# The delta rule's scan in chunks of 128 tokens instead of 64, its triangle's inverse doubled once more, the decays' mask as a factor

## The chip, the cores and the metric

The kernel runs on one core of one Trainium2 chip. The metric is the device time of one execution in microseconds (us); before the change it is 1946.99 us, the median of three runs (1946.99 to 1947.81). The engines are called TensorE (PE in the profile, PEld for its weight loads), VectorE (DVE), ScalarE (ACT), GpSimd (POOL) and SyncE (SP, a DMA queue).

## The reference, cut to what matters

The program is four layers one after another over 512 tokens of width 1024: two of attention and long convolution, then two hybrid layers. Each hybrid layer has three branches: a gated delta rule with 4 heads of 128x128 state, a latent attention with 8 heads, and a linear recurrence (LRU). Only the delta rule is touched by the change:

```python
def gated_delta_rule(q, k, v, g, beta):      # chunks of C = 64 tokens in the reference
    gc = cumsum(g) within the chunk
    decay = exp(where(tril, gc[i] - gc[j], -inf))
    a_mat = where(strict_tril, (k*beta) @ k.T * decay, 0) + eye(C)
    u, w = triangular_solve(a_mat, [v*beta, k*beta*exp(gc)])
    attn = where(tril, q @ k.T * decay, 0)
    for each chunk n:
        v_new = u - w @ state
        o     = (q * exp(gc)) @ state + attn @ v_new
        state = state * exp(g_last) + (k * exp(g_last - gc)).T @ v_new
```

The result does not depend on the chunk's length in exact arithmetic: a longer chunk means a larger triangle to invert and fewer steps of the loop.

## The kernel before, in words

Tokens lie in 4 tiles of 128 partitions (index i), heads are c = 0 to 3. A projection is 8 x 3 matmuls of 512 columns (lines 261 to 263, `mm3`: high and low parts of the operands), and accumulates in one of three PSUM buffers, which `ps("acc")` hands out in turn as acc, acc, fl (lines 233 to 244). Other PSUM tags are lg (2 buffers), tr and ft (1 each, in turn) and av (1). Big SBUF tiles of 128x4x512 come from `U()`, one pool whose number of buffers is the first argument of `k.pools(10, dict(acc=2, fl=1, lg=2, tr=1, ft=1, av=1))` (lines 222 and 1591). Weights pass through `wchunk`: one DMA on SyncE, a copy on ScalarE (line 269), a difference on VectorE or GpSimd (line 270), three buffers of each.

The order on each engine is not written out by hand. A planner (Tile) takes the instructions in program order as priorities, simulates the engines and lets an instruction whose operands and buffers are ready go ahead of earlier ones that wait; the queues then run in that fixed order. A tile takes a buffer of its pool when the planner lets its first writer go, and gives it back after its last reader.

A hybrid layer (`layer2`, line 1502) runs in program order:

- `mla_pre` (line 1010) makes the compressed keys `ckv` (a U tile) and the decays' logarithms g.
- `gdn_front` (line 1242): `sums` and `decay` make exp of the decays in `an`: a product of the mask `ml` with g on GpSimd (line 1266), an fp32 matmul by `ms` (1268), a second matmul that adds `negr`, which is -1e30 outside the 64x64 triangles (1269), and an exponential on ScalarE (1270). Then 12 projections make k2, q2 and v2 (U tiles), with a convolution on VectorE (`conv4`, line 990) and, for the keys, scales on GpSimd (1289 to 1295) and the triangle `at` (1305).
- `solve32` (line 1356), placed in the program before the last query projection: the sixteen 32x32 diagonal blocks go to DRAM and back (ScalarE's DMA queue, 1360 and 1364) into a U tile `w`, whose second half is cleared on GpSimd (1365); 31 steps of two VectorE instructions invert all blocks (1371, 1373); the result goes to DRAM (`dm`, 1374), its transpose is made on ScalarE (1375) and goes to DRAM too (`dmt`, 1376).
- `spread` (line 1384): twelve DMAs on ScalarE's queue bring the inverted blocks back as `xc` and `xtc` (two tiles tagged "go") and on the diagonal of `XT` (cleared on GpSimd, 1390).
- `gdn_inv` (line 1398), per tile of 128 tokens: two products on TensorE (1406, 1412) with copies on ScalarE (1408, 1414) make the off-diagonal 32x32 block of each 64x64 triangle; then `wt` and `un` (1418, 1422).
- `gdn` (line 1430): the gate `gz`, a U tile, is made of four projections, each emptied by a tanh on ScalarE and a product on VectorE (`silu2`, lines 703 and 704). Then the scan: for each tile i and each half n of 64 tokens, per pair of heads q: two matmuls by the state (1462), a difference on VectorE (1463), two for the queries (1465), two for the state's update (1470), the decayed state on GpSimd (1473) and its sum on VectorE (1474). After both halves `later` and the tile's output (1479 to 1497).
- `lru` (line 1174): per c a projection with a convolution (987, 990), gates through av (1204, 1207), a scan, a second projection and the output `o`, a U tile, written on GpSimd (1223).
- `mla_v`, `mla`, then `out2`.

Of the kernel before, what the change touches and what calls it, by code (L numbers as in the profile page):

```python
# [51 lines left out]
def shape_constants():  # L52
    c = {}
    i = np.arange(256)
    cas = lambda w: np.stack([np.cos(w) + np.sin(w), np.cos(w) - np.sin(w)], 1)
    m = np.arange(P)
    th = np.pi * (4 * i + 1) / 2048
    ph = 2 * np.pi * (((2 * m[:, None] + 1) * (4 * i[None, :] + 1)) % 2048) / 2048
    fwd = cas(ph)
    c["fwd"] = np.stack(_f32r(fwd))  # L60
    f = np.where(i < P, np.cos(th), np.sin(th)) ** 2 / 1024.0
    inv = (fwd * f).reshape(P, 2, 2, P).transpose(3, 2, 1, 0)
    c["inv"] = np.ascontiguousarray(inv, np.float32)
    d = np.concatenate([np.arange(q, S, 4) for q in (0, 2, 1, 3)])
    w = 2 * np.pi * ((m[:, None, None] * 2 + np.arange(2)[:, None]) * (4 * m + 1) % 1024) / 1024
    flt = np.stack(_f32r(np.stack([np.cos(w), np.sin(w)], 2)))
    c["fltb"] = flt.reshape(2, P, 4, P)
    c["rot"] = np.stack([np.tan(th[:P]), -np.tan(th[:P]), 1.0 / np.tan(th[P:]), np.cos(2 * th[:P]), np.sin(2 * th[:P])],
                        1).astype(np.float32)
    tt = np.arange(S, dtype=np.float32) * np.float32(1 / 511)  # L70
    tres = np.arange(S, dtype=np.float32)
    f = np.linspace(1e-4, 15, 16, dtype=np.float32)
    ang = ((np.float32(2.0 * math.pi) * tres)[:, None] * f[None, :]) / np.float32(S)
    z = np.concatenate([tt[:, None], np.cos(ang), -np.sin(ang)], axis=-1).astype(np.float32)
    c["zt"] = np.ascontiguousarray(z[d].T)
    c["negt"] = np.ascontiguousarray(-tt[d].reshape(4, P).T)
    kill = np.zeros((P, 1), np.float32)
    kill[0, 0] = NEG
    c["kill"] = kill
    rel = np.arange(-511, 512)  # L80
    n = np.abs(rel)
    large = 7 + sum((n >= v).astype(np.int64) for v in (8, 12, 16, 23, 32, 46, 64, 91))
    bucket = np.where(rel > 0, 16, 0) + np.where(n < 8, n, large)
    onehot = np.zeros((32, 1024), np.float32)
    onehot[bucket, 1022 - np.arange(1023)] = 1.0
    c["onehot"] = onehot
    ang = np.arange(S, dtype=np.float32)[:, None] * np.array(ROPE_INV, np.uint32).view(np.float32)[None, :]
    co, si = np.cos(ang.astype(np.float64)).T, np.sin(ang.astype(np.float64)).T
    c["cos"] = np.concatenate([co] * 4).astype(np.float32)
    c["sin"] = np.concatenate([-si, si, -si, si]).astype(np.float32)  # L90
    p = np.arange(P)
    same = (p[:, None] // 64) == (p[None, :] // 64)
    le = p[:, None] <= p[None, :]
    c["ml"] = (same & le).astype(np.float32)
    c["ms"] = (same & (p[:, None] > p[None, :])).astype(np.float32)
    c["mc"] = np.stack([np.repeat((p // 64 == n)[:, None], P, 1) for n in range(2)], 1).astype(np.float32)
    c["neg"] = np.where(same & le, 0.0, NEG).astype(np.float32)
    i, j = p[None, :] >> 5, p[:, None] >> 5
    c["lv"] = (((i >> 1) == (j >> 1)) & (i & 1 == 1) & (j & 1 == 0)).astype(np.float32)
    c["causal"] = np.concatenate([np.zeros((P, 384)), np.where(le.T, 0.0, NEG)], 1).astype(np.float32)  # L100
    return c

# [69 lines left out]
class Kern:  # L172
# [789 lines left out]

    def setup2(self):
        nc, A = self.nc, self.A
        for n, shape in (("ml", [P, P]), ("ms", [P, P]), ("mc", [P, 2, P]), ("lv", [P, P])):
            setattr(self, n, self.load(self.cq, n, shape))
        self.negr = self.cq.tile([P, P], F32R, tag="negr", name="negr")
        nc.gpsimd.dma_start(self.negr, A["neg"])
        self.idr = self.cq.tile([P, P], F32R, tag="idr", name="idr")
        nc.scalar.activation(self.idr, self.ident, AF.Copy)  # L970
        self.ones = self.cq.tile([P, 1], F32, tag="ones", name="ones")
        nc.gpsimd.memset(self.ones, 1.0)
        d = lambda n: [self.dp.tile([64, 1024], F32, tag=f"{n}{l}", name=f"{n}{l}") for l in range(2)]
        self.da, self.dm, self.dmt = d("da"), d("dm"), d("dmt")
# [267 lines left out]
    def gdn_front(self, l, h, gab):  # L1242
# [10 lines left out]

        kn, kbt = self.T("XT", four), self.T("X", four)
        quad = lambda n, tag: self.sm(4 * n, tag).rearrange("p (i c) -> p i c", i=4)
        eg, sc, rk, ssq = quad(16, "eg"), quad(16, "sc"), quad(4, "rk"), quad(4, "ssq")
        ones = self.ones
        nc.gpsimd.tensor_scalar(sc[:, :, 12:16], bt, 0.5, None, op0=MUL)
        by = lambda t: t.unsqueeze(2).to_broadcast([P, 4, P])
        tile = lambda i: slice(i * P, (i + 1) * P)  # L1260
# [2 lines left out]
        def decay(i):  # L1263

            rg = self.T("g2", (P, 4, P))
            nc.gpsimd.tensor_tensor(rg, self.mbc(self.ml), self.bc(g[:, i]), op=MUL)
            pd = self.ps("lg", (P, 4, P))
            mm(pd, self.ms, rg, start=True, stop=False)
            mm(pd, self.idr, self.mbc(self.negr), start=False, stop=True)
            nc.scalar.activation(an[:, i], pd, AF.Exp)  # L1270

        def sums():

            pg = self.ps("lg", (P, 4, 16))
            for n, m in enumerate((self.ml, self.ms, self.mc[:, 0], self.mc[:, 1])):
                mm(pg[:, n], m, g.rearrange("p i c -> p (i c)"), start=True, stop=True)
            nc.scalar.activation(eg.rearrange("p i (n c) -> p n i c", n=4), pg.rearrange("p n (i c) -> p n i c", i=4), AF.Exp)

        def keys(c, sq):
            pk = self.ps("tr", (P, 4, P))  # L1280
# [103 lines left out]
    def spread(self, l):  # L1384


        nc = self.nc
        xc, xtc = (self.T("go", (P, 16, 32)) for _ in range(2))
        XT = self.T("XT", (P, 4, 4, P))
        nc.gpsimd.memset(XT, 0.0)  # L1390
        for k in range(4):
            rs = slice(32 * k, 32 * k + 32)
            nc.scalar.dma_start(xc[rs], self.blk(self.dm[l], k))
            nc.scalar.dma_start(xtc[rs], self.blk(self.dmt[l], k))
            nc.scalar.dma_start(self.diag(XT, k), self.blk(self.dmt[l], k))
        return xc, xtc, XT

    def gdn_inv(self, i, at, t1, X, kb, v2):

        nc = self.nc  # L1400
        mm = nc.tensor.matmul
        ts = slice(i * P, (i + 1) * P)
        xc, xtc, XT = X
        p1 = self.ps("lg", (P, 4, 32))
        for c in range(4):
            mm(p1[:, c], at[:, i, c], xc[:, 4 * i + c], start=True, stop=True)
        for b in (0, 64):
            nc.scalar.activation(t1[b + 32:b + 64, i, :, b:b + 32], p1[b + 32:b + 64], AF.Copy)
        yield
        p2 = self.ps("tr", (P, 4, 32))  # L1410
        for c in range(4):
            mm(p2[:, c], t1[:, i, c], xtc[:, 4 * i + c], start=True, stop=True)
        for b in (0, 64):
            nc.scalar.activation(XT[b:b + 32, i, :, b + 32:b + 64], p2[b:b + 32], AF.Copy, scale=-1.0)
        yield
        pw = self.ps("lg", (P, 4, P))
        for c in range(4):
# [12 lines left out]
    def gdn(self, l, h, q2, k2, v2, at, an, kb, egs, ssq, t1, X):  # L1430
# [19 lines left out]
        for i in range(4):  # L1450
            ts = slice(i * P, (i + 1) * P)
            eg = egs[:, i]
            po = self.ps("tr", (P, 4, P))
            for n in range(2):
                rs = slice(64 * n, 64 * n + 64)
                cs = slice(i * P + 64 * n, i * P + 64 * n + 64)
                for q in range(2):
                    hs = slice(2 * q, 2 * q + 2)
                    s1 = st[q]
                    ps = self.ps("lg", (P, 2, P))  # L1460
                    for c in range(2):
                        mm(ps[rs, c], wt[:, i, 2 * q + c, rs], s1[:, c], start=True, stop=True)
                    nc.vector.tensor_tensor(un[rs, hs, ts], un[rs, hs, ts], ps[rs], op=SUB)
                    for c in range(2):
                        mm(po[rs, 2 * q + c], q2[:, 2 * q + c, cs], s1[:, c], start=True, stop=True)
                for q in range(2):
                    hs = slice(2 * q, 2 * q + 2)
                    pS = self.ps("lg", (P, 2, P))
                    for c in range(2):
                        mm(pS[:, c], kd[rs, 2 * q + c, ts], un[rs, 2 * q + c, ts], start=True, stop=True)  # L1470
                    s2 = self.T("st", (P, 2, P))
                    e = eg[:, 8 + 4 * n + 2 * q:10 + 4 * n + 2 * q]
                    nc.gpsimd.tensor_tensor(s2, st[q], e.unsqueeze(2).to_broadcast([P, 2, P]), op=MUL)
                    nc.vector.tensor_tensor(s2, s2, pS, op=ADD)
                    st[q] = s2
                if n == 0:
                    later()
            o = self.T("go", (P, 4, P))
            nc.vector.tensor_tensor(o, po, self.bc(eg[:, 0:4]), op=MUL)
            p2 = self.ps("tr", (P, 4, P))  # L1480
# [135 lines left out]
```

## Time and profile before

| what | us |
|---|---|
| median of three runs | 1946.99 |
| profiled execution | 1947.53 |
| its span on the core | 1945.8 |
| TensorE busy | 1882.4 (97%) |
| VectorE busy | 1290.4 (66%) |
| ScalarE busy | 890.0 (46%) |
| GpSimd busy | 648.2 (33%) |

The span is what the profile sees of the profiled execution; its device time is 1.7 us longer. Busy time of TensorE is not work at its peak: matmuls are pipelined, and a row's duration overlaps the next row's. What one costs in a full stream is the time from its start to the start of the next row. A number after "x" is how many instructions a row merges. The two hybrid layers run from about 960 to 1450 and from 1450 to the end, with the same pattern.

### The profile page before, as it was taken

What the parts mean: (1) busy time and instruction counts of PE and PEld (TensorE: products, weight loads), DVE (VectorE), ACT (ScalarE), POOL (GpSimd) and SP (SyncE); (2) the same over time, 40 slices, a digit from 0 to 9 for tenths busy, and PEclk for the clock granted to TensorE, in tenths of its full rate; (3) what the DMA queues carried; (4) which work ended last, traced back from release to release, by engine and by line L of the source; (5) the groups of instructions that cost most, each with busy time, mean ns of one, the idle gap of its engine ahead of it and who ended that gap; (6) DMA issues with size and microseconds to landing.
All of it is one profiled execution on the core that took longest, in us unless ns stands there. A gap on an engine that the chain in (4) does not pass through costs nothing.

```text
span 1945.8 us, 26168 instructions
## 1 busy us (share of the span) xinstructions
PE 1882.4 (97%) x9632; PEld 1566.2 (80%) x9632; DVE 1290.4 (66%) x2278; ACT 890.0 (46%) x1732; POOL 648.2 (33%) x555
## 2 busy tenths in 40 slices
PE   8997999999998899999999999999999999999998
PEld 5886888888787687888888777788889887778886
DVE  5887698634697868873558866667334886666732
ACT  4765322234475632233346254466334625446631
POOL 2544344433243634442235314211013532421111
PEclk9999999999999999999999999999999999999999
DMA  5331433324323242323432231112333223121232
GB/s 180 106 121 64 146 109 98 105 91 163 117 86 113 73 170 89 112 93 104 135 123 75 81 101 39 63 44 77 138 127 107 75 87 95 38 63 47 83 130 87
DMA packets 88393, 192.35 MB, mean 99 GB/s; under 512 B 28258, under 2 KB 38499, under 8 KB 88265
## 3 DMA queue, kind: packets, MB, share of 16 engines
q1 hardware_dynamic: 69592, 184.84, 29.0%
q10 hardware_dynamic: 17376, 3.67, 1.0%
q0 software_dynamic: 1296, 2.16, 0.4%
q8 instruction: 76, 1.25, 0.3%
q14 instruction: 53, 0.43, 0.1%
HBM read 172.28 MB, written 18.37 MB: 98 GB/s over the span
## 4 chain that ended last, share of the span: by engine, by line
PE 65%; DVE 11%; issue 3%; ACT 2%; DMA 1%; POOL 1%; ACTq 1%; POOLq 0%; DVEq 0%; SPq 0%
PE acc L261 11%; PE acc L263 11%; PE acc L262 11%; PE fl L261 5%; PE fl L262 5%; PE fl L263 5%; PE av L1166 2%; DVE u L1373 1%; DVE s L1371 1%; PE av L261 1%; PE av L262 1%; PE av L263 1%; PE lg L1470 1%; DVE wl L270 1%; PE av L820 1%
## 5 line engine op out<-in xcount | busy, mean ns | idle before, releaser
L269 ACT ACTIVATE wh<-wr 128x1024 fp32r<-128x1024 f32 (+3 forms) x268 | 256.1, 956 | 467.5 <-PE acc L262 231.3
L261 PE MATMUL acc<-u,wh 128*128 128x512 f32 x1000 | 400.6, 401 | 3.2 <-DVE o L704 1.9
L262 PE MATMUL acc<-u,wh 128*128 128x512 f32 x1000 | 400.4, 400 | 0.0
L263 PE MATMUL acc<-u,wl 128*128 128x512 f32 x1000 | 397.8, 398 | 0.0
L270 POOL TENSOR_TENSOR wl<-wr,wh 128x1024 fp32r<-128x1024 f32 (+3 forms) x86 | 187.2, 2177 | 555.2 <-ACT wh L269 460.2
L270 DVE TENSOR_TENSOR wl<-wr,wh 128x1024 fp32r<-128x1024 f32 (+3 forms) x182 | 213.3, 1172 | 184.8 <-ACT wh L269 182.6
L261 PEld LDWEIGHTS acc<-u,wh 128*128 128x128 f32 x1000 | 190.8, 191 | 46.1 <-issue 3.3
L263 PEld LDWEIGHTS acc<-u,wl 128*128 128x128 f32 x1000 | 190.9, 191 | 43.6 <-issue 4.9
L262 PEld LDWEIGHTS acc<-u,wh 128*128 128x128 f32 x1000 | 190.8, 191 | 39.8 <-issue 2.3
L261 PE MATMUL fl<-u,wh 128*128 128x512 f32 x312 | 124.4, 399 | 0.0
L263 PE MATMUL fl<-u,wl 128*128 128x512 f32 x312 | 122.7, 393 | 0.0
L262 PE MATMUL fl<-u,wh 128*128 128x512 f32 x312 | 122.2, 392 | 0.0
L263 PE MATMUL acc<-wh,u 128*128 128x512 f32 (+1 forms) x212 | 79.3, 374 | 0.3
L262 PE MATMUL acc<-wl,u 128*128 128x512 f32 (+1 forms) x212 | 79.4, 374 | 0.0
L261 PE MATMUL acc<-wh,u 128*128 128x512 f32 (+1 forms) x212 | 77.8, 375 | 0.4 <-ACT u L269 0.2
L261 PEld LDWEIGHTS fl<-u,wh 128*128 128x128 f32 x312 | 58.7, 188 | 12.8 <-issue 1.6
L679 ACT ACTIVATE p<-p,mx 128x512 f32<-128x512 f32 x64 | 45.7, 717 | 49.9 <-DVE mx L677 49.9
L263 PEld LDWEIGHTS fl<-u,wl 128*128 128x128 f32 x312 | 58.6, 188 | 12.1
L262 PEld LDWEIGHTS fl<-u,wh 128*128 128x128 f32 x312 | 58.7, 188 | 12.0 <-issue 0.8
L324 ACT ACTIVATE sq<-x 128x512 f32<-128x512 f32 x40 | 25.2, 631 | 61.4 <-DVE x L1569 38.4
L793 POOL TENSOR_TENSOR w<-w,ab 128x256 f32<-128x256 f32 x32 | 33.5, 1047 | 57.9 <-DVE w L792 53.1
L902 POOL TENSOR_TENSOR m<-m,u 128x512 f32<-128x512 f32 x16 | 24.7, 1546 | 66.3 <-DVE m L901 66.3
(610 smaller groups left out, 4473.8 us busy)
## 6 DMA issues: line engine op xcount, KB each, us to landing
wr<-in_win SPq DMA_DIRECT2D x88, 512.0 KB, 3.4
wr<-in_xin SPq DMA_DIRECT2D x64, 512.0 KB, 3.4
wr<-in_xout SPq DMA_DIRECT2D x32, 512.0 KB, 3.5
hd<-f SPq DMA_DIRECT2D x32, 256.0 KB, 2.4
hs<-hd SPq DMA_DIRECT2D x32, 256.0 KB, 3.4
wr<-in_wout SPq DMA_DIRECT2D x16, 512.0 KB, 3.5
xd<-x SPq DMA_DIRECT2D x12, 512.0 KB, 2.9
x<-xd SPq DMA_DIRECT2D x12, 512.0 KB, 3.9
```

The lines of the kernel that those rows point to most:

```text
L261: mm(ps, l[0], r[0], start=first, stop=False)
L262: mm(ps, l[0], r[1], start=False, stop=False)
L263: return mm(ps, l[1], r[0], start=False, stop=last)
L269: nc.scalar.activation(hi, src, AF.Copy)
L270: (nc.gpsimd if pool else nc.vector).tensor_tensor(lo, src, hi.bitcast(F32), op=SUB)
L324: self.nc.scalar.activation(self.T("sq"), self.xt(i)[:, h * S:(h + 1) * S], AF.Square, scale=1.0 / math.sqrt(D), accum_out=self.ms2[i][:, ...
L679: nc.scalar.activation(pp[c], pp[c], AF.Exp, bias=mx[:, c:c + 1], accum_out=s0[:, i:i + 1] if c == 0 else s)
L793: nc.gpsimd.tensor_tensor(a[:, 0], a[:, 0], b[:, 1], op=ADD)
L820: nc.tensor.matmul(ps[:, k], Y[j][:, k, cs], iv[:, j, (k + 1) // 2 % 2], start=j == 0, stop=j == 1)
L902: nc.gpsimd.tensor_tensor(m, m, ma[f // 4][:, f % 4], op=ADD)
L1166: mm(po[:, ts], v[hd // 4][:, k, (hd % 4) * P:(hd % 4 + 1) * P], w[:, k], start=k == 0, stop=k == i)
L1371: nc.vector.tensor_tensor(t, a[:, j, c:].unsqueeze(2).to_broadcast([64, r, c]), m[:, j:j + 1, :c].to_broadcast([64, r, c]), op=MUL)
```

## The change

The chunks become 128 tokens, one tile i: the masks `ml`, `ms` and the eg sums lose their division into halves (`mc` goes, `ones` becomes a full 128x128 tile); the matmul that added -1e30 goes, and `an` is multiplied by `ml` on GpSimd after the exponential. `spread` builds `xd` (a U tile, 128x16x96, cleared on GpSimd) with the first three diagonal blocks in place of `xc`. `gdn_inv` gets two more rounds: the first product is 96 columns wide, a second product in the second round puts the lower off-diagonal block into `xd`, and two 64-column products make the 64x64 off-diagonal block of the 128x128 inverse. The scan's loop over halves goes; each pair of heads takes full 128-row tiles, and the last tile makes no new state.

```diff
--- before.py
+++ after.py
@@ -89,14 +89,11 @@
     c["cos"] = np.concatenate([co] * 4).astype(np.float32)
     c["sin"] = np.concatenate([-si, si, -si, si]).astype(np.float32)
     p = np.arange(P)
-    same = (p[:, None] // 64) == (p[None, :] // 64)
     le = p[:, None] <= p[None, :]
-    c["ml"] = (same & le).astype(np.float32)
-    c["ms"] = (same & (p[:, None] > p[None, :])).astype(np.float32)
-    c["mc"] = np.stack([np.repeat((p // 64 == n)[:, None], P, 1) for n in range(2)], 1).astype(np.float32)
-    c["neg"] = np.where(same & le, 0.0, NEG).astype(np.float32)
+    c["ml"] = le.astype(np.float32)
+    c["ms"] = (p[:, None] > p[None, :]).astype(np.float32)
     i, j = p[None, :] >> 5, p[:, None] >> 5
-    c["lv"] = (((i >> 1) == (j >> 1)) & (i & 1 == 1) & (j & 1 == 0)).astype(np.float32)
+    c["lv"] = (((i >> 1) == (j >> 1)) & (i & 1 == 1) & (j & 1 == 0) | (i >> 1 == 1) & (j >> 1 == 0)).astype(np.float32)
     c["causal"] = np.concatenate([np.zeros((P, 384)), np.where(le.T, 0.0, NEG)], 1).astype(np.float32)
     return c
 
@@ -962,13 +959,9 @@
 
     def setup2(self):
         nc, A = self.nc, self.A
-        for n, shape in (("ml", [P, P]), ("ms", [P, P]), ("mc", [P, 2, P]), ("lv", [P, P])):
-            setattr(self, n, self.load(self.cq, n, shape))
-        self.negr = self.cq.tile([P, P], F32R, tag="negr", name="negr")
-        nc.gpsimd.dma_start(self.negr, A["neg"])
-        self.idr = self.cq.tile([P, P], F32R, tag="idr", name="idr")
-        nc.scalar.activation(self.idr, self.ident, AF.Copy)
-        self.ones = self.cq.tile([P, 1], F32, tag="ones", name="ones")
+        for n in ("ml", "ms", "lv"):
+            setattr(self, n, self.load(self.cq, n, [P, P]))
+        self.ones = self.cq.tile([P, P], F32, tag="ones", name="ones")
         nc.gpsimd.memset(self.ones, 1.0)
         d = lambda n: [self.dp.tile([64, 1024], F32, tag=f"{n}{l}", name=f"{n}{l}") for l in range(2)]
         self.da, self.dm, self.dmt = d("da"), d("dm"), d("dmt")
@@ -1253,8 +1246,8 @@
 
         kn, kbt = self.T("XT", four), self.T("X", four)
         quad = lambda n, tag: self.sm(4 * n, tag).rearrange("p (i c) -> p i c", i=4)
-        eg, sc, rk, ssq = quad(16, "eg"), quad(16, "sc"), quad(4, "rk"), quad(4, "ssq")
-        ones = self.ones
+        eg, sc, rk, ssq = quad(12, "eg"), quad(16, "sc"), quad(4, "rk"), quad(4, "ssq")
+        ones = self.ones[:, 0:1]
         nc.gpsimd.tensor_scalar(sc[:, :, 12:16], bt, 0.5, None, op0=MUL)
         by = lambda t: t.unsqueeze(2).to_broadcast([P, 4, P])
         tile = lambda i: slice(i * P, (i + 1) * P)
@@ -1265,16 +1258,16 @@
             rg = self.T("g2", (P, 4, P))
             nc.gpsimd.tensor_tensor(rg, self.mbc(self.ml), self.bc(g[:, i]), op=MUL)
             pd = self.ps("lg", (P, 4, P))
-            mm(pd, self.ms, rg, start=True, stop=False)
-            mm(pd, self.idr, self.mbc(self.negr), start=False, stop=True)
+            mm(pd, self.ms, rg, start=True, stop=True)
             nc.scalar.activation(an[:, i], pd, AF.Exp)
+            nc.gpsimd.tensor_tensor(an[:, i], an[:, i], self.mbc(self.ml), op=MUL)
 
         def sums():
 
-            pg = self.ps("lg", (P, 4, 16))
-            for n, m in enumerate((self.ml, self.ms, self.mc[:, 0], self.mc[:, 1])):
+            pg = self.ps("lg", (P, 3, 16))
+            for n, m in enumerate((self.ml, self.ms, self.ones)):
                 mm(pg[:, n], m, g.rearrange("p i c -> p (i c)"), start=True, stop=True)
-            nc.scalar.activation(eg.rearrange("p i (n c) -> p n i c", n=4), pg.rearrange("p n (i c) -> p n i c", i=4), AF.Exp)
+            nc.scalar.activation(eg.rearrange("p i (n c) -> p n i c", n=3), pg.rearrange("p n (i c) -> p n i c", i=4), AF.Exp)
 
         def keys(c, sq):
             pk = self.ps("tr", (P, 4, P))
@@ -1385,33 +1378,49 @@
 
 
         nc = self.nc
-        xc, xtc = (self.T("go", (P, 16, 32)) for _ in range(2))
+        xtc = self.T("go", (P, 16, 32))
+        xd = self.U((P, 16, 96))
         XT = self.T("XT", (P, 4, 4, P))
         nc.gpsimd.memset(XT, 0.0)
+        nc.gpsimd.memset(xd, 0.0)
         for k in range(4):
             rs = slice(32 * k, 32 * k + 32)
-            nc.scalar.dma_start(xc[rs], self.blk(self.dm[l], k))
+            if k < 3:
+                nc.scalar.dma_start(xd[rs, :, rs], self.blk(self.dm[l], k))
             nc.scalar.dma_start(xtc[rs], self.blk(self.dmt[l], k))
             nc.scalar.dma_start(self.diag(XT, k), self.blk(self.dmt[l], k))
-        return xc, xtc, XT
+        return xd, xtc, XT
 
     def gdn_inv(self, i, at, t1, X, kb, v2):
 
         nc = self.nc
         mm = nc.tensor.matmul
         ts = slice(i * P, (i + 1) * P)
-        xc, xtc, XT = X
-        p1 = self.ps("lg", (P, 4, 32))
+        xd, xtc, XT = X
+        p1 = self.ps("lg", (P, 4, 96))
         for c in range(4):
-            mm(p1[:, c], at[:, i, c], xc[:, 4 * i + c], start=True, stop=True)
+            mm(p1[:, c], at[:, i, c], xd[:, 4 * i + c], start=True, stop=True)
         for b in (0, 64):
-            nc.scalar.activation(t1[b + 32:b + 64, i, :, b:b + 32], p1[b + 32:b + 64], AF.Copy)
+            nc.scalar.activation(t1[b + 32:b + 64, i, :, b:b + 32], p1[b + 32:b + 64, :, b:b + 32], AF.Copy)
         yield
-        p2 = self.ps("tr", (P, 4, 32))
+        p2 = self.ps("tr", (P, 2, 4, 32))
         for c in range(4):
-            mm(p2[:, c], t1[:, i, c], xtc[:, 4 * i + c], start=True, stop=True)
+            mm(p2[:, 0, c], XT[:, i, c], t1[:, i, c, 0:32], start=True, stop=True)
+        for c in range(4):
+            mm(p2[:, 1, c], t1[:, i, c], xtc[:, 4 * i + c], start=True, stop=True)
+        nc.scalar.activation(xd[32:64, 4 * i:4 * i + 4, 0:32], p2[32:64, 0], AF.Copy, scale=-1.0)
         for b in (0, 64):
-            nc.scalar.activation(XT[b:b + 32, i, :, b + 32:b + 64], p2[b:b + 32], AF.Copy, scale=-1.0)
+            nc.scalar.activation(XT[b:b + 32, i, :, b + 32:b + 64], p2[b:b + 32, 1], AF.Copy, scale=-1.0)
+        yield
+        p3 = self.ps("lg", (P, 4, 64))
+        for c in range(4):
+            mm(p3[:, c], at[:, i, c], xd[:, 4 * i + c, 0:64], start=True, stop=True)
+        nc.scalar.activation(t1[64:128, i, :, 0:64], p3[64:128], AF.Copy)
+        yield
+        p4 = self.ps("tr", (P, 4, 64))
+        for c in range(4):
+            mm(p4[:, c], t1[:, i, c], XT[:, i, c, 64:128], start=True, stop=True)
+        nc.scalar.activation(XT[0:64, i, :, 64:128], p4[0:64], AF.Copy, scale=-1.0)
         yield
         pw = self.ps("lg", (P, 4, P))
         for c in range(4):
@@ -1451,30 +1460,25 @@
             ts = slice(i * P, (i + 1) * P)
             eg = egs[:, i]
             po = self.ps("tr", (P, 4, P))
-            for n in range(2):
-                rs = slice(64 * n, 64 * n + 64)
-                cs = slice(i * P + 64 * n, i * P + 64 * n + 64)
-                for q in range(2):
-                    hs = slice(2 * q, 2 * q + 2)
-                    s1 = st[q]
-                    ps = self.ps("lg", (P, 2, P))
-                    for c in range(2):
-                        mm(ps[rs, c], wt[:, i, 2 * q + c, rs], s1[:, c], start=True, stop=True)
-                    nc.vector.tensor_tensor(un[rs, hs, ts], un[rs, hs, ts], ps[rs], op=SUB)
-                    for c in range(2):
-                        mm(po[rs, 2 * q + c], q2[:, 2 * q + c, cs], s1[:, c], start=True, stop=True)
-                for q in range(2):
-                    hs = slice(2 * q, 2 * q + 2)
-                    pS = self.ps("lg", (P, 2, P))
-                    for c in range(2):
-                        mm(pS[:, c], kd[rs, 2 * q + c, ts], un[rs, 2 * q + c, ts], start=True, stop=True)
-                    s2 = self.T("st", (P, 2, P))
-                    e = eg[:, 8 + 4 * n + 2 * q:10 + 4 * n + 2 * q]
-                    nc.gpsimd.tensor_tensor(s2, st[q], e.unsqueeze(2).to_broadcast([P, 2, P]), op=MUL)
-                    nc.vector.tensor_tensor(s2, s2, pS, op=ADD)
-                    st[q] = s2
-                if n == 0:
-                    later()
+            for q in range(2):
+                hs = slice(2 * q, 2 * q + 2)
+                s1 = st[q]
+                ps = self.ps("lg", (P, 2, P))
+                for c in range(2):
+                    mm(ps[:, c], wt[:, i, 2 * q + c], s1[:, c], start=True, stop=True)
+                nc.vector.tensor_tensor(un[:, hs, ts], un[:, hs, ts], ps, op=SUB)
+                for c in range(2):
+                    mm(po[:, 2 * q + c], q2[:, 2 * q + c, ts], s1[:, c], start=True, stop=True)
+            for q in range(2 if i < 3 else 0):
+                pS = self.ps("lg", (P, 2, P))
+                for c in range(2):
+                    mm(pS[:, c], kd[:, 2 * q + c, ts], un[:, 2 * q + c, ts], start=True, stop=True)
+                s2 = self.T("st", (P, 2, P))
+                e = eg[:, 8 + 2 * q:10 + 2 * q]
+                nc.gpsimd.tensor_tensor(s2, st[q], e.unsqueeze(2).to_broadcast([P, 2, P]), op=MUL)
+                nc.vector.tensor_tensor(s2, s2, pS, op=ADD)
+                st[q] = s2
+            later()
             o = self.T("go", (P, 4, P))
             nc.vector.tensor_tensor(o, po, self.bc(eg[:, 0:4]), op=MUL)
             p2 = self.ps("tr", (P, 4, P))
```

## Rows read from the trace of the kernel before

**Rows 1.** The page's head: span, and busy us (share) xinstructions of each engine.
```profile
span 1945.8 us, 26168 instructions
PE 1882.4 (97%) x9632; PEld 1566.2 (80%) x9632; DVE 1290.4 (66%) x2278; ACT 890.0 (46%) x1732; POOL 648.2 (33%) x555
```

**Rows 2.** Windows of both delta layers: stretch, length, busy PE, PEld, DVE, ACT, POOL, PEclk, DMA.
```profile
1091.00:1111.20 20.20, 18.06 (x85) 14.45 (x84) 19.86 (x37) 5.77 (x8) 3.46 (x2) 1.00 0.33 105
1111.20:1140.00 28.80, 28.35 (x121) 22.46 (x121) 23.27 (x48) 9.38 (x10) 2.39 (x1) 1.00 0.38 103
1140.00:1167.00 27.00, 25.96 (x167) 22.42 (x166) 14.49 (x15) 20.47 (x38) 7.03 (x6) 0.94 0.32 81
1167.00:1253.00 86.00, 86.00 (x450) 64.66 (x449) 55.48 (x84) 38.46 (x75) 33.08 (x32) 1.00 0.16 47
...
1595.70:1625.00 29.30, 28.23 (x121) 22.11 (x120) 23.36 (x49) 8.66 (x10) 2.71 (x2) 1.00 0.41 112
```

**Rows 3.** Timeline of TensorE in the scan: start us, us, engine line op, names, shapes.
```profile
1167.32 0.65 PE L1462 MATMUL lg<-st,kb 128*64 128x128 f32 x4
1167.90 0.50 PE L262 MATMUL fl<-u,wh 128*128 128x512 f32 x1
...
1170.73 1.09 PE L1465 MATMUL ft<-st,u 128*64 128x128 f32 x8
1171.75 0.50 PE L261 MATMUL fl<-u,wh 128*128 128x512 f32 x1
...
1173.80 1.16 PE L1470 MATMUL lg<-u,u 64*128 64x128 f32 x8
1174.88 0.51 PE L263 MATMUL fl<-u,wl 128*128 128x512 f32 x1
```

**Rows 4.** Timeline of TensorE in the blocks' inverse.
```profile
1140.26 1.87 PE L1406 MATMUL lg<-go,at 128*128 128x32 f32 x16
1141.96 0.48 PE L261 MATMUL acc<-u,wh 128*128 128x512 f32 x1
...
1162.73 1.95 PE L1418 MATMUL lg<-XT,kb 128*128 128x128 f32 x16
1164.51 1.06 PE L1422 MATMUL ft<-u,XT 128*128 128x128 f32 x8
```

**Rows 5.** Timeline of TensorE where the third gate projection ends.
```profile
1111.01 0.39 PE L263 MATMUL acc<-u,wl 128*128 128x512 f32 x1
1111.24 0.39 PE L261 MATMUL fl<-u,wh 128*128 128x512 f32 x1
```

**Rows 6.** Timeline of GpSimd during the keys.
```profile
1047.95 1.05 POOL L1293 TENSOR_TENSOR go<-XT,sc 128x512 f32<-128x512 f32 x1
1048.94 0.95 POOL L1365 MEMSET u<- 64x1024 f32 x1
```

**Rows 7.** Timeline of ScalarE and its DMA queue (ACTq), from the solve on.
```profile
1099.11 0.58 ACT L703 ACTIVATE u<-fl 128x512 f32<-128x512 f32 x1
...
1134.78 0.45 ACTq L1376 DMA_DIRECT2D dmt<-u  x1
...
1138.51 0.31 ACTq L1394 DMA_DIRECT2D go<-dmt  x1
...
1142.10 0.52 ACTq L1395 DMA_DIRECT2D XT<-dmt  x1
...
1145.52 1.12 ACT L1408 ACTIVATE X<-lg 32x128 f32<-32x128 f32 x4
```

**Rows 8.** Timeline of VectorE in the solve.
```profile
1116.97 0.67 DVE L704 SCALAR_TENSOR_TENSOR u<-u,acc 128x512 f32<-128x512 f32 x1
...
1128.28 0.73 DVE L990 SCALAR_TENSOR_TENSOR lu<-acc,c,lu 128x511 f32<-128x511 f32 x1
...
1131.87 0.18 DVE L1373 TENSOR_TENSOR u<-u,s 64x31 f32<-64x31 f32 x1
```

**Rows 9.** Windows in an earlier layer (columns as in rows 2).
```profile
624.00:631.00 7.00, 5.93 (x15) 4.49 (x15) 3.06 (x7) 0.29 (x1) 1.02 (x1) 0.55 0.34 111
```

## The prediction

> **What bounds the kernel now.** I read the page's busy shares first, then stretches of the first delta layer, then the order of work on each engine inside them. TensorE is busy for 1882.4 of 1945.8 us [rows 1], so a change counts for the TensorE time that it removes and for the idle time that it opens. The stretches show where the delta rule lies [rows 2]: from 1091 to 1140 VectorE runs the 32x32 solve (19.86 of 20.20 us busy, then 23.27 of 28.80) while TensorE is kept full by projections that don't depend on it (28.35 of 28.80 us from 1111.2 on); from 1140 to 1167 the blocks' inverse; from 1167 to 1253 the scan, 86.00 of 86.00 us busy. The second layer repeats this (28.23 of 29.30 us in its second half of the solve). Everywhere the gaps of the delta chain are filled with other projections, so the chain's latency is not paid today.
>
> **TensorE's work, part by part (one layer).**
> *Scan.* An fp32 matmul is two passes. A group of four passes with 64 columns of weights takes 0.58 us from its start to the next row, eight passes of the query product 1.02, eight with 64 rows 1.08 [rows 3]. Eight steps with two pairs of heads each: 16 x (0.58 + 0.51 + 0.54) = 26.1 us. Afterwards there are four steps of full tiles, the last without a state update: 8 + 8 + 6 = 22 groups of four. Sixteen full passes take 1.78 us [rows 4], 0.45 us a group; with the lead-in that a lone group pays in rows 3 it is up to 0.58. I take 0.53: 11.7 us, a saving of 14.4 (13.3 to 16.2).
> *Decays.* Four 512-column mask matmuls at 0.23 us (the step between the two rows of [rows 5]) go: 0.9. One of four tiny sums goes: 0.2.
> *Inverse.* Per tile of 128 tokens the first product only grows from 32 to 96 columns. Sixteen passes of 32 columns take 1.70 us and of 128 columns 1.78 [rows 4], so width is free here. Three products of four heads are new: 4 x 3 x 4 x 2 = 96 passes at 0.106 to 0.111: 10.4 us.
> Net: -14.4 - 0.9 - 0.2 + 10.4 = -5.1 us a layer.
>
> **Other engines.** GpSimd gains four 128x512 products (1.05 us) and one clearing of 1536 columns; one of 1024 took 0.95 us [rows 6], so 1 to 1.5 us. It loses 10 of 16 state products. VectorE loses more than half of the scan's updates. ScalarE gains three copies per tile of 128 tokens. All of it lies beside a full TensorE at no cost, as long as TensorE is full; without that cover GpSimd's additions, which stand ahead of the keys' scales in its order, could delay the solve by up to 5 us.
>
> **Where the cover breaks: the big buffers.** The pool behind U has ten. When the solve runs, h's four, the compressed keys' one, q2, k2 and v2 are live: eight. The solve's w is the ninth; it is cleared at 1048.94 and read until the store of the transposed inverse, issued at 1134.78 [rows 6, 7]. The gate gz is the tenth: it is written from 1099.11 on, while w is still live [rows 7]. The pool is full. The change takes the new xd from the same pool (it was a small "go" tile), ahead of gz in program order, and xd's first writer is a clearing that waits for nothing; w's clearing ran 35 us ahead of the solve in the same way. So xd gets the tenth buffer and gz has to wait until w is stored.
> What queues behind it: a gate's projection goes into one of the three accumulators acc, acc, fl, and is emptied by a tanh that writes gz. With gz unavailable the first three gate projections fill all three. The fourth gate and the recurrence's convolutions need the same accumulators; nothing else is ready. The third gate projection ends at 1111.24 [rows 5]. From there TensorE has nothing to do for what today are 28.35 busy us.
> *When it resumes.* The solve ends at 1132.05 [rows 8]. The four gate products and three convolution steps on VectorE that now fall inside it (0.67 and 0.73 us [rows 8]) move behind it: -4.5, so 1127.5. From its end to the freed buffer: the store is issued 2.7 us after the end and over 0.45 later, and its first reader starts 6.5 us after the end [rows 7]; between 3.2 and 6.5, I take 6, near the reader: 1133.5. Tanh and gate product, 0.58 and 0.67 us [rows 7, 8]: 1134.8. If ScalarE issues the spread's eight remaining DMAs first (0.52 each [rows 7]), 4.1 us later. That is 23.6 to 27.7 us idle, less up to 3.5 us for the 32 passes of the first inverse product, which need no accumulator: 20 to 27. I take 24, less the 0.45 us that are idle there now: +23.5 us a layer.
> Here the Trainium skill ("Perfetto Trace Analysis", Identifying Performance Opportunities) says that a gap which repeats on the engine that should be saturated can mean that SBUF or PSUM has no room for the next tile. By that rule the gap is to be looked for at these buffers, and the sum is the one below; if only work counted, it would be the first rival's. The trace of before shows no such gap in this stretch, so no run has tested it here.
>
> **The clock.** After TensorE's pauses near 620 us, the stretch 624 to 631 was granted 0.55, the 1.2 GHz level instead of 2.4 for almost all of it [rows 9]: 7 us that did the work of some 3.9. The inverse's stretch has 0.94 of 27 us now, 1.6 us lost [rows 2]. A long pause should give one more such stretch, a loss between nothing and 3.5 us, or take the place of the present one (-1.6); I take +1.5 a layer.
> The Trainium skill's "TensorE: Matmul & The Clock Gate" (HAM oscillation) states the same direction: idle gaps throttle the array and the next work starts cold.
>
> **Sum.** Per layer -5.1 + 23.5 + 1.5 = +19.9, twice: +39.8. The profiled execution took 1947.53 us around its span of 1945.8, and the median of the three runs is 1946.99: 1947.5 + 39.8 = 1987.3, on the median's footing 1987.
>
> **The rivals.**
> 1. *Only the work counts*: gz gets its buffer in time, or the wait is covered, and 2 x 5.1 us are saved: 1937. For it: TensorE is 97% busy and the scan's groups are dear. Against it: ten live tiles, counted. Chance 0.10.
> 2. *A short starvation*: projections of the recurrence get accumulators before the gates, and some 14 of the 24 us are filled: 2 x (10 - 5.1 + 1) = +12: 1959. For it: the planner places work by what is ready. Against it: the gates come first in the program, and before it ran them first. Chance 0.13.
> 3. *A deeper one*: the recurrence's output is the next tile from U and must now wait for xd, that is for the third inverse product; and two more rounds go through ScalarE, where the first product's copies began 5.3 us after its passes did [rows 4, 7]. Up to 5 us a round and two rounds, +10 a layer: 2007. Chance 0.10.
> 4. *The two cancel* within 4 us: 0.02.
> The forecast, 1970 to 2000, has 0.65. The first rival is the one on the other side: it decides as soon as the idle time per layer is under 5.1 us.
>
> **How the numbers follow.** The range 1955 to 2006 takes in the forecast, the second rival and the near half of the third; the first rival and the far tail, about 0.17, are left out. Faster by over 0.2% (4 us, about what can be told from no change): the first rival, 0.10. Within: 0.02. Slower: 0.88.
>
> **What would show it.** In the trace after: the tanh that writes gz (u<-fl, u<-acc) starts only after the store of the transposed inverse instead of 35 us before it; TensorE shows one gap of 20 us or more per delta layer, between the third gate projection and that tanh, and the clock's half level behind it; the scan's three lines together fall from about 26 to about 12 us a layer, and the inverse grows by about 10. The forecast is wrong if gz is written during the solve, or if TensorE's idle time in the solve's stretch stays near today's 2.6 us; if the gap is there and the time is still near 1945, the scan's saving was far larger than 14 us a layer.

## The result, and the profile after

The changed kernel takes 1999.47 us (median of four runs, 1998.49 to 2000.63) against 1946.99 us for the kernel before (four runs, 1946.33 to 1947.81): 1.027 times the time, with a 95% interval of 1.0252 to 1.0287. The prediction was 1987, with a range of 1955 to 2006. Its sign, its main mechanism (the wait for a buffer) and the place of that wait are in the trace; two of its terms, the clock and the work, were far off, in opposite directions.

This is the page of the kernel after: the head, busy us by engine, and two rows of the 40 slices (about 50 us each).

```profile
span 1997.4 us, 26076 instructions
PE 1887.7 (95%) x9604; PEld 1590.8 (80%) x9604; DVE 1281.2 (64%) x2242; ACT 896.5 (45%) x1755; POOL 648.8 (32%) x544
...
PE   8997999999998999999999599999999959999998
...
PEclk9998999999999999999999679999999977999999
```

TensorE has slightly more busy time than before [rows 1], in 28 instructions fewer. The slices show why: twice it is half idle, and in these slices and the ones behind them the granted clock (PEclk, in tenths of 2.4 GHz) is down. Windows of the first delta layer after, with the columns of [rows 2]:

```profile
1091.00:1108.00 17.00, 15.36 (x71) 12.16 (x69) 16.69 (x33) 5.33 (x7) 3.66 (x2) 1.00 0.40 121
1108.00:1130.00 22.00, 0.19 (x1) 0.22 (x2) 13.76 (x38) 2.46 (x2) 0.00 (x0) 0.58 0.26 62
1130.00:1155.00 25.00, 25.00 (x116) 24.81 (x117) 1.88 (x3) 7.49 (x25) 0.00 (x0) 0.50 0.12 19
1155.00:1180.00 25.00, 25.00 (x141) 23.48 (x141) 0.43 (x1) 8.25 (x17) 0.00 (x0) 0.71 0.00 1
1180.00:1200.00 20.00, 20.00 (x121) 17.37 (x120) 11.91 (x22) 5.89 (x14) 6.72 (x6) 1.00 0.21 64
```

Where [rows 2] had 28.35 of 28.80 us busy, TensorE now works 0.19 of 22.00 us. Then follow 40 us in which it is busy all the time, at a granted clock of 0.50: the 1.2 GHz level. "Busy" hides that half of these 40 us is lost.

GpSimd clears xd before the solve starts, and so xd holds its big buffer from then on:

```profile
1080.76 1.38 POOL L1385 MEMSET u<- 128x1536 f32 x1
```

TensorE's timeline across the pause (start, us, engine, line, operation, names; in brackets the idle time before and what ended it):

```profile
1107.27 0.39 PE L260 MATMUL acc<-u,wl 128*128 128x512 f32 x1
1129.81 1.56 PE L1402 MATMUL lg<-u,at 128*128 128x96 f32 x6 [22.16 <-DMA u<-dm]
```

The pause ends with the first product of the inverse, which waits for the spread's DMA into xd and needs no accumulator. ScalarE and its DMA queue (ACTq) there:

```profile
1122.92 0.47 ACTq L1367 DMA_DIRECT2D dm<-u  x1
...
1125.40 0.45 ACTq L1369 DMA_DIRECT2D dmt<-u  x1
1125.89 1.93 ACTq L1389 DMA_DIRECT2D u<-dm  x3
...
1131.94 0.50 ACTq L1391 DMA_DIRECT2D XT<-dmt  x1
1132.49 0.55 ACT L1404 ACTIVATE X<-lg 32x128 f32<-32x128 f32 x2 [7.12 <-DMA go<-dmt]
1133.06 0.60 ACT L700 ACTIVATE u<-fl 128x512 f32<-128x512 f32 x1
1133.56 1.08 ACT L700 ACTIVATE u<-acc 128x512 f32<-128x512 f32 x2
```

The three tanhs that write gz stand at 1133.06 to 1134.6, all behind the store of w's transposed inverse (1125.40) and behind the spread's DMAs on the same queue. In [rows 7] the first of them starts 35.7 us before that store. The second delta layer has the same pause, 22.27 us from 1622.23 on.

I split the span of both kernels by TensorE's rows: pauses of over 1 us; for all other rows the time from one start to the next, multiplied by the granted clock (work at full clock), and what the lower clock adds to it. The split is of one profiled execution of each kernel. In us for the whole execution, with the rest (under 0.5) left out:

| | before | after | difference | predicted |
|---|---|---|---|---|
| pauses over 1 us | 30.3 | 77.8 | +47.5 | +47.0 |
| added by the 1.2 GHz level | 15.9 | 44.3 | +28.4 | +3.0 |
| all passes but the projections', at full clock | 378.1 | 355.1 | -23.0 | -10.2 |
| 6743 passes of the projections, at full clock | 1506.4 | 1505.6 | -0.8 | 0 |

So the change does save TensorE work, more than twice what I had reckoned. It pays for it with a pause and with a low clock behind the pause.

### The profile page after: what moved, and what is told of

Read it like the earlier page. It is cut to its first block, busy times and chain, and to the rows that moved or that the text cites. A ratio compares the mean times of both kernels' runs of the same rounds, so it can differ in the third digit from the quotient of the medians.

```text
span 1997.4 us, 26076 instructions
## 1 busy us (share of the span) xinstructions
PE 1887.7 (95%) x9604; PEld 1590.8 (80%) x9604; DVE 1281.2 (64%) x2242; ACT 896.5 (45%) x1755; POOL 648.8 (32%) x544
## 4 chain that ended last, share of the span: by engine, by line
PE 63%; DVE 11%; issue 3%; ACT 3%; POOL 2%; DMA 2%; ACTq 0%; SPq 0%; POOLq 0%; DVEq 0%
PE acc L260 10%; PE acc L258 10%; PE acc L259 10%; PE fl L260 5%; PE fl L258 5%; PE fl L259 5%; PE av L1159 2%; DVE s L1364 1%; DVE u L1366 1%; PE av L259 1%; PE av L258 1%; PE av L260 1%; DVE wl L267 1%; PE av L817 1%; PE lg L260 1%
## 5 line engine op out<-in xcount | busy, mean ns | idle before, releaser
L258 PE MATMUL fl<-u,wh 128*128 128x512 f32 x312 | 125.7, 403 | 0.0
L259 PE MATMUL fl<-u,wh 128*128 128x512 f32 x312 | 125.7, 403 | 0.0
L1478 POOL TENSOR_TENSOR st<-st,eg 128x256 f32<-128x256 f32 x12 | 10.1, 847 | 164.3 <-DVE st L1479 164.3
L1402 PE MATMUL lg<-u,at 128*128 128x96 f32 x64 | 14.8, 426 | 44.4 <-DMA u<-dm 44.4
```

Source lines behind the costliest of these rows:

```text
L258: mm(ps, l[0], r[0], start=first, stop=False)
L259: mm(ps, l[0], r[1], start=False, stop=False)
L1402: mm(p1[:, c], at[:, i, c], xd[:, 4 * i + c], start=True, stop=True)
```

## The experiments

My theory before the runs: xd takes the last of ten big buffers, gz waits for w, and the pause pulls the clock down. The rivals: the pause has another cause; the added small passes hold the clock down by themselves; the next tile from the pool waits in its turn.

**e1: w out of the pool.** The solve's w goes into the buffer that t1 uses later, so the pool has room for xd and gz.

```
-        w = self.U()[0:64].rearrange("p (n a) (b i) -> p n (a b) i", n=2, i=32)
+        w = self.T("X", (P, 4, S))[0:64].rearrange("p (n a) (b i) -> p n (a b) i", n=2, i=32)
...
-                    t1 = self.T("X", four)
-                    nc.gpsimd.memset(t1, 0.0)
                     self.solve32(l, at)
+                    t1 = self.T("X", four)
+                    nc.gpsimd.memset(t1, 0.0)
```

> The changed kernel, but the solve's w takes the buffer that t1 gets later (X) instead of one of the ten big buffers, so that xd and gz both find one. Theory (the tenth buffer): the pause of 22.2 us a layer goes, gz is written during the solve again; the small passes that the change saves (11.5 us a layer at full clock in the trace after) are left: 1947 - 23 = 1924, with the clock low for a few us a layer as before; 1920 to 1932. Rival 1 (the clock): the inverse's 96 added small passes hold TensorE at 1.2 GHz whether or not a pause came before; then 18.2 and 11.8 us stay lost: about 1953. Rival 2 (the next buffer): the recurrence's output o now waits for xd until the third product of the inverse, a new pause of up to 10 us a layer: about 1944. Rival 3 (the pause has another cause than the pool): it stays, 1999.

Measured: 1929.22 us, 0.9909 (0.9893 to 0.9926) of the kernel before (1946.8 in these rounds). The window that was empty is full again, and the inverse runs mostly at full clock:

```profile
1107.00:1130.00 23.00, 22.76 (x101) 18.59 (x100) 22.00 (x48) 5.89 (x7) 2.75 (x2) 1.00 0.30 101
1130.00:1155.00 25.00, 23.18 (x124) 18.68 (x123) 11.70 (x14) 13.34 (x25) 7.26 (x5) 0.93 0.49 117
1155.00:1180.00 25.00, 25.00 (x160) 22.56 (x160) 10.11 (x10) 14.13 (x27) 4.42 (x5) 0.86 0.08 25
```

The theory's forecast holds, and three rivals fall: the pause is the pool's; the wait of the recurrence's output o opens no pause of more than 1.6 us; and the new small passes alone don't keep the clock at 1.2 GHz. The wait of o does exist, on GpSimd: o's first product waits 4.93 us for the third product of the inverse (L1417), the last reader of xd.

```profile
1168.56 1.27 POOL L1216 TENSOR_TENSOR u<-l,l 128x512 f32<-128x512 f32 x1 [4.93 <-PE lg L1417]
```

By the split, the low level adds 8.5 us in the two delta layers here, 3.4 before. This difference is not shown to come from the small passes: the mean granted clock of e1's five executions lies between 0.986 and 0.989, which is itself some 6 us, and e7 below has the same passes and 3.4 us. An eleventh buffer in the pool itself was not run.

**e2: the pool's part alone, in the kernel before.** Scan, inverse and mask are the old ones; only xc becomes a big tile that is cleared early.

```
-        xc, xtc = (self.T("go", (P, 16, 32)) for _ in range(2))
+        xtc = self.T("go", (P, 16, 32))
+        xc = self.U((P, 16, 32))
...
+        nc.gpsimd.memset(xc, 0.0)
```

> The kernel before, with only its xc (16x32) taken from the pool of ten big buffers and cleared, as the change does with xd: scan, inverse and decays stay those of before. Theory: the pool alone makes the pause, 20 to 23 us a layer of TensorE idle time between the third gate projection and the inverse, so +42 us; with a clock that stays at 1.2 GHz through the old inverse as it did through the new one, another 15 to 28 us: 2004 to 2017. Rival (the clock stays low only because of the change's added small passes): +42 and 1 to 5 us: 1990 to 1994. Rival (the pause needs the longer chain of the change): 1947.

Measured: 1991.13 us, 1.0233 (1.0218 to 1.0249). TensorE around the pause, and where its clock returns:

```profile
1108.52 0.39 PE L263 MATMUL acc<-u,wl 128*128 128x512 f32 x1
1131.17 1.06 PE L1408 MATMUL lg<-u,at 128*128 128x32 f32 x4 [22.26 <-DMA u<-dm]
```

```profile
1138.71 0.77 PE L261 MATMUL fl<-u,wh 128*128 128x512 f32 x1
1139.28 0.63 PE L262 MATMUL fl<-u,wh 128*128 128x512 f32 x1
...
1141.84 0.60 PE L262 MATMUL fl<-u,wh 128*128 128x512 f32 x1
1142.27 0.41 PE L263 MATMUL fl<-u,wl 128*128 128x512 f32 x1
```

The pause needs nothing of the change but one more tile of the pool: 22.26 and 21.98 us. But my theory's figure for the clock (2004 to 2017) was wrong here, and the rival's (1990 to 1994) was right. With the old inverse the low level ends within a row of projection passes, at 1142.3 (the pass then takes 0.41 instead of 0.63 us); it adds 10.3 us in the two layers, where the changed kernel has 33.4. So pause and small passes act together in the changed kernel: the pause brings the clock down, and it stays down through the longer run of small passes behind it.

**e3: the pause filled.** The wait is as it was, but TensorE streams through it.

```
...
+            if c == 2:
+                for n in range(88):
+                    mm(ps, self.zr, h[n % 8][0], start=False, stop=n == 87)
             self.silu2(gz[:, c], ps)
```

> The changed kernel, with 88 more passes of 512 columns and zero weights at the end of the third gate projection, 20.0 us a layer that add nothing to the result; the wait for the buffer stays as it is. Theory (the idle pause is what drops the clock): no time is lost or won by the passes themselves, but TensorE enters the inverse at 2.4 GHz, and of the 28 us that the lower level costs in the trace after most come back: 1999 - 28 = 1971, 1965 to 1980. Rival (the small passes of the inverse hold the clock down by themselves): 1995 to 2003. Rival (the passes come in the way of other work): over 2005.

Measured: 1978.97 us, 1.0166 (1.0151 to 1.0181), inside the theory's 1965 to 1980.

```profile
1107.36 20.11 PE L1457 MATMUL acc<-u,zr 128*128 128x512 f32 x88
1129.93 2.08 PE L1404 MATMUL lg<-u,at 128*128 128x96 f32 x16 [2.46 <-DMA u<-dm]
```

40 us of passes that compute nothing make the changed kernel 20 us faster: what the low level adds falls from 44.3 to 22.3 us in all. A run that fills an idle engine with useless work is a good way to price a clock.

**e5: streams behind the pause.** The pause stays; 20 wide passes come behind the first four products of the inverse.

```
...
+        if i == 0:
+            for n in range(20):
+                mm(p1.rearrange("p c i -> p (c i)"), self.zr, h[n % 8][0][:, 0:384], start=False, stop=n == 19)
...
```

> The changed kernel with its pause; behind the first four products of the inverse 20 more passes of 384 columns with zero weights run, that add nothing to the result. Theory (after a pause the clock stays at 1.2 GHz as long as only small passes with gaps between the columns run, and a run of wide passes brings it back): the clock rises within some 6 us of the inverse's start, at 1136 instead of 1169 and 1651 instead of 1671. The added passes cost 3.4 us a layer at full clock, the lost time in the inverse falls from 18.2 and 11.8 us to 4 to 8 each: 1999 + 7 - 16 = 1990, 1982 to 1996. Rival (the length of the pause or a fixed time sets the return, whatever runs): the clock rises as late as before, 2006 to 2013.

Measured: 1979.70 us, 1.017 (1.0155 to 1.0185). The rival is out, but the theory's size missed too: 1979.70 is under its range of 1982 to 1996.

```profile
1132.03 1.99 PE L1404 MATMUL lg<-u,at 128*128 128x96 f32 x8 [22.44 <-DMA u<-dm]
1133.73 5.36 PE L1407 MATMUL lg<-u,zr 128*128 128x384 f32 x20
1138.93 1.03 PE L1404 MATMUL lg<-u,at 128*128 128x96 f32 x8
1139.74 0.48 PE L258 MATMUL fl<-u,wh 128*128 128x512 f32 x1
```

The same eight products take 1.99 us ahead of the 20 passes and 1.03 behind them. The record of the granted clock has the return at 1137.32, within these passes, against 1169.66 in the kernel after; in all the low level adds 24.4 us instead of 44.3. In e3 and e5 the planner also puts more projection passes between the products, so their gain is that of the added passes and of this order together; I did not separate the two.

**e4: the mask alone.** The kernel before without the product with negr, the mask as a factor on GpSimd.

```
-            mm(pd, self.ms, rg, start=True, stop=False)
-            mm(pd, self.idr, self.mbc(self.negr), start=False, stop=True)
+            mm(pd, self.ms, rg, start=True, stop=True)
             nc.scalar.activation(an[:, i], pd, AF.Exp)
+            nc.gpsimd.tensor_tensor(an[:, i], an[:, i], self.mbc(self.ml), op=MUL)
```

> The kernel before, with only the decays' mask changed: the product with negr is left out and the mask is a factor on GpSimd. By the prediction's 0.23 us a product: -1.8 us, 1945.2. By the rows of the trace of before (four products with a start-to-start time of 0.554 us): -4.4 us, 1942.6. Rival (GpSimd's four more products a layer delay the keys and with them the solve): slower, up to 1957.

Measured: 1944.45 us, 0.9985 (0.9976 to 0.9994), that is -4.7 to -1.2 us. The rival falls: GpSimd's four products a layer don't make the kernel slower; whether they take back a part of the gain this can't tell. The interval holds both -4.4 and -1.8, so it doesn't choose between the two prices; the rows do (below).

**e6: e1 without the third and fourth product of the inverse.** The block that couples the two halves of 128 tokens is not computed.

```
-        p3 = self.ps("lg", (P, 4, 64))
...
-        nc.scalar.activation(XT[0:64, i, :, 64:128], p4[0:64], AF.Copy, scale=-1.0)
-        yield
```

> The kernel of e1_w_elsewhere (w outside the ten big buffers), with the third and the fourth product of the inverse left out, so that the block that couples the two halves of 128 tokens is not computed. By the prediction's price (64 of its 96 added passes at 0.106 us): -6.8 us a layer, 1929 - 13.6 = 1915.6. Rival 1 (these passes also keep the clock low: 8.5 us are lost in the delta layers of e1, 3.4 before): up to 5 us more, 1910. Rival 2 (they lie where TensorE would wait for ScalarE's copies anyway): 1925 to 1929.

Measured: 1917.74 us (four executions, 1913.43 to 1922.46), 11.5 less than e1 (13.6 by the prediction's price). By the split the work outside the projections falls by 12.5 us, from 356.0 in e1 to 343.5. Most of the passes' price is paid, so they are on the path; the waits for ScalarE's copies between them don't hide them.

**e7: the gates first.** All tiles stay where the change put them; the loop of the four gate projections is moved ahead of the spread in the program, so gz is the first to ask for the tenth buffer.

```
-        X = self.spread(l)
         self.busy = False
+        gz = self.U()
+        for c in range(4):
+            ps = self.ps("acc")
+            self.projT(self.wchunk(A[f"xin{l}"][12 + c], 8, P), h, ps)
+            self.silu2(gz[:, c], ps)
+        X = self.spread(l)
...
```

> The changed kernel with all its tiles where they are, but the four gate projections come ahead of the spread in the program, so that gz takes the tenth big buffer and xd has to wait for w. Theory (who claims the tenth buffer decides): gz is written during the solve and the pause of 22 us goes; xd's clearing (1.38 us) and the spread come after the store of w, 2 to 5 us later than in e1, behind projections: 1925 to 1938. Rival 1 (the late spread opens a pause of its own of 5 us or more a layer): 1940 to 1950. Rival 2 (eleven tiles for ten buffers, whoever claims): 1999.

Measured: 1922.98 us, 0.9882 (0.9865 to 0.9898): the fastest version that computes the whole result, ahead of both kernels, and 2 us under the theory's range of 1925 to 1938. Two rows of its profile, ScalarE's first tanh of gz and GpSimd's clearing of xd:

```profile
1099.24 0.58 ACT L700 ACTIVATE u<-fl 128x512 f32<-128x512 f32 x1
```

```profile
1132.86 1.38 POOL L1390 MEMSET u<- 128x1536 f32 x1 [12.62 <-DMA dmt<-u]
```

gz is written at 1099.24 again (1099.11 in [rows 7]), and the wait is now xd's: its clearing ends the wait for the store of w, at 1132.86. TensorE has projections for that time; its longest pause in the two delta layers is 1.44 us. What the low level adds there is 3.4 us, as before. o waits for xd here too, on GpSimd, 22.0 us over both layers, and TensorE shows no pause for it.

**e8: the order of e7 in the kernel before.** The edit is that of e7.

> The kernel before, with only the order of e7 (the four gate projections ahead of the spread in the program). Theory (the order is worth something only where eleven tiles want ten buffers): no difference, 1943 to 1951. Rival (the order itself saves what e7 gained over e1, 6 us): 1941 or less. Rival (the order costs, and e7 would gain more without it): over 1951.

Measured: 1945.72 us, 0.9998 (0.9989 to 1.0008). The order is worth nothing that can be measured where ten tiles have ten buffers, so e7's 24 us against the kernel before are the change's own saving.

## Why the prediction came out as it did

*The buffers: right.* Eleven live tiles want ten buffers, xd comes first, and three gate projections fill three accumulators. The idle time was 22.2 us a layer (24 predicted, 23.5 net). That the length came out so near is in part luck, since two errors went the same way. The pause begins at 1107.7, where I had put it at 1111.2. The solve runs from 1082.7 to 1122.9 (before, from 1084.3 to 1132.1), and I had let it end at 1127.5; the seven VectorE steps that I moved behind it add up to 4.9 us, not to the 4.5 that I took, and the solve became 7.6 us shorter. Why the start and the end both come earlier, no run separates. The order I named as dear, the spread's DMAs ahead of the tanh, came true: the tanh starts 7.7 us after the store was issued. The first product's passes, which need no accumulator, had then been running for 3.3 us, as I had allowed for. The Trainium skill ("Perfetto Trace Analysis", Identifying Performance Opportunities) reads a gap that repeats on the engine that should be saturated as a possible lack of room for the next tile; e1, e2 and e7 bear that out here.

*The clock: the step that failed.* I took "+1.5 a layer" because the only example of a long pause [rows 9] was followed by 7 us at the low level, and gave it a bound of 3.5. It measured +18.2 and +11.8 us. In [rows 9] projections follow the pause; here the inverse follows it, small passes for the most part: 1129.81 to 1169.66 and 1644.5 to 1671.42 went by at 1.2 GHz. In the first layer five projection passes from 1157.96 on were not yet followed by the full clock; it came back after a row of them from 1166.92 to 1169.63, where a pass takes 0.41 us instead of 0.63:

```profile
1153.27 3.23 PE L1417 MATMUL lg<-u,at 128*128 128x64 f32 x14
1156.29 1.91 PE L1422 MATMUL ft<-XT,X 128*128 128x64 f32 x8
1157.96 0.77 PE L260 MATMUL fl<-u,wl 128*128 128x512 f32 x1
...
1160.24 1.80 PE L1417 MATMUL lg<-u,at 128*128 128x64 f32 x8
...
1165.25 2.02 PE L1427 MATMUL lg<-XT,kb 128*128 128x128 f32 x8
1166.92 0.77 PE L259 MATMUL fl<-u,wh 128*128 128x512 f32 x1
...
1169.20 0.61 PE L258 MATMUL fl<-u,wh 128*128 128x512 f32 x1
1169.63 0.41 PE L259 MATMUL fl<-u,wh 128*128 128x512 f32 x1
```

The pauses ahead of [rows 9] were shorter too (3.11 us the longest), but that alone is not the step: e2, with a pause of 22 us and the old inverse, loses 3.9 and 3.1 us a layer more than before, close to my bound. What I had wrong was to price the pause without the work that TensorE does after it, and the prediction had the list of that work in hand. The Trainium skill ("TensorE: Matmul & The Clock Gate", HAM oscillation) has the direction, a cold start after an idle gap, and the traces agree; its size they had to show.

*The work: right in sign, too small by half.* Per layer, by start-to-start time at full clock: the scan's three lines fell from 25.6 to 9.1 us, -16.4 instead of -14.4 and just outside my 13.3 to 16.2. A group of four takes 0.42 us (22 groups in 9.14), not 0.53; its rows in the scan after:

```profile
1179.32 0.61 PE L1468 MATMUL lg<-st,kb 128*128 128x128 f32 x4
1179.76 0.61 PE L1471 MATMUL ft<-st,u 128*128 128x128 f32 x4
1180.21 0.61 PE L1468 MATMUL lg<-st,kb 128*128 128x128 f32 x4
```

The mask's four products were worth 2.2, not 0.9: I took the 0.23 us of a projection pass from [rows 5], but this product's own start-to-start time in the trace of before is 0.554 in the mean of eight. One of them there:

```profile
1018.70 0.79 PE L1269 MATMUL lg<-negr,idr 128*128 128x512 f32 x1
1019.33 0.39 PE L263 MATMUL acc<-u,wl 128*128 128x512 f32 x1
```

The inverse added 10.0 (10.4 predicted). A further 1.9 lie in the products and transposes around it (L1418, L1422, L1482 and L1496 before, 13.8 us; 12.0 after), which I had left at no change. Together that is -10.5 of the -11.5 us a layer; the rest is spread over small groups.

*The sum.* Over both layers the work came out 13.6 us below my figure and the clock 25.4 us above it. What is left of the two is 12 us. That the time fell into the range is luck: with my figure for the work, the clock's cost would have put it near 2013. One term of three, the pause, had the right size.

*The rivals.* "Only the work counts" is what e1 and e7 show once gz has its buffer in time: 1929 and 1923. I had given it 1937, because of the work's size. "A deeper starvation" came nearest in time (2007), but not by its mechanism: o does wait for xd in e1 and e7, for 9.4 and 22.0 us over both layers, but on GpSimd and at no cost to TensorE, and the profile of the changed kernel itself shows no such wait.

## What to carry to other kernels

Count the live tiles of a pool before and after a change. One tile too many costs whatever the displaced tile was feeding, and e2 shows the price here (44 us) with none of the gain. Who asks first is a choice: e7 moves the same wait to a tile that can afford it, and turns +2.7% into -1.2%. Where a pause is opened on TensorE, price the work behind it at the low clock too: here the small passes behind the pause ran at it for 27 to 40 us, and 20 wide passes a layer put ahead of most of them (e5, with the order that the planner then made) took 20 us off the kernel.

## What the runs showed of the hardware that was not expected

Behind a pause of 22 us TensorE was busy in every window of 1130 to 1169.6 and stayed at a granted 0.50:

```profile
1130.00:1150.00 20.00, 20.00 (x93) 19.81 (x94) 1.88 (x3) 6.43 (x21) 0.00 (x0) 0.50 0.15 23
1150.00:1169.60 19.60, 19.60 (x82) 18.57 (x82) 0.00 (x0) 3.75 (x11) 0.00 (x0) 0.50 0.00 1
1169.60:1185.00 15.40, 15.40 (x109) 14.21 (x108) 3.08 (x5) 5.99 (x10) 0.00 (x0) 1.00 0.11 35
```

The profile's "busy" was thus no sign that the clock was back or about to be; in e5 it was back some 30 us earlier, within 20 wide passes. And passes that compute nothing can pay: 176 of them in e3 took 40 us of TensorE's pauses and gave back 22 us of clock.
